# Another written-out order of the tasks between the first tiles and the first FFN

## The chip, the cores and the metric

The kernel runs on one core of a Trainium2 chip. The metric is the device time of one execution in microseconds (us). A core has five engines with a queue of instructions each: TensorE (PE: matmuls and transposes), VectorE (DVE), ScalarE (ACT), GpSimd (POOL) and SyncE (SP, which issues most transfers). An engine works through its own queue in order; between engines, semaphores say when an operand is ready or a buffer free. So the order in which a program writes its instructions is, for each engine, the order in which they run, and an instruction that waits holds up all that stand behind it.

## The reference

Two layers on 512 positions of width 1024 in float32. Each layer is a token mixer and a SwiGLU FFN; each of the four is wrapped as below, with shift, scale and gate computed from a conditioning vector c.

```
def residual_update(x, c, ada_w, ada_b, ln_g, ln_b, sublayer):
    shift, scale, gate = ada_modulation(c, ada_w, ada_b)
    out = sublayer(x * (1 + scale) + shift)
    return layer_norm(ALPHA * x + (1 + gate) * out, ln_g, ln_b)
```

The mixer of layer 0, in which the change lies, makes one input projection (q, keys and values of three branches, gates, and u and v of a gated MLP). Sparse attention with 8 query heads and 2 groups of keys takes compressed blocks of 32 positions, selected blocks of 64 (here all of them: 8 blocks, of which up to 16 may be chosen) and a window of 512, and adds the three results with a gate per head. Beside it a spatial gate computes u * (tril(W_s) norm(v) + b) in chunks of 128 positions. Both together go through one output projection:

```
    o_nsa = nsa_attention(q, *kv, gates, cmp_pos, cmp_w1, cmp_w2)
    o_gmlp = chunked_gmlp(u, v, gmlp_norm_g, gmlp_ws, gmlp_bs)
    return jnp.concatenate([o_nsa, o_gmlp], axis=-1) @ w_out
```

The mixer of layer 1 is a short gated convolution; an FFN is `(silu(gate) * up) @ w_out` with 2816 hidden columns.

## The kernel before

The 512 positions are four row tiles of 128 (t = 0 to 3). Float32 products are made of three matmuls: weights and activations are split into a high half (ScalarE, L469) and the rest (raw minus high, L473, on VectorE or GpSimd), called hi and lo, and a product is hi*hi + lo*hi + hi*lo. Such a split of half a weight unit (128x1024) is called a conversion here; for the output projections a fold (L459) multiplies the weights by a gate first.

The program has three parts: the first tiles (with an order of its own, ORDER_0), the stage between them and the first FFN, and the rest: first FFN, layer 1 and second FFN. The change is in the stage, about 60 to 304 us of the profile. What it does there: the compression of keys and values (L1054); the rest of the input projection by row tiles (L1331); the gating norm (mean L1361, centring L1366, variance L1374, an inverse square root by Newton steps over all row tiles at once, L1389 to L1397, then apply L1401 and gain L1406); the spatial-gate matmul (L1445) with its evacuation (L1449); its turn into columns (L1474) with a high half (L1482) and a low half (L1484); attention; and the output projection (L533), each piece of which is evicted into the residual by VectorE (L538).

Attention goes by units, from the last row tile to the first and through the two key groups: unit (3,0), (3,1), (2,0) down to (0,1); "V" and the numbers name a unit's value part. A unit has score heads (L1520, L1569) with a masked maximum on VectorE (L1528), exponentials on ScalarE (L1599), sums and scales by 1/sum (L1605, L1606, and L1611 on GpSimd or L1617 on ScalarE). Its compressed scores are then turned on TensorE (L1670) into a bank, split into a high half (L1673, ScalarE) and a low half (L1676, VectorE) and multiplied with the compressed values (L1680). The same is done block by block with the other scores: turn (L1693), high (L1698), low (L1702), product (L1707, L1708). Banks are scarce: two for turns, one for products of values, one for pieces of the output projection. At the end of a unit an add (L1738) and a split (L1746, L1749) give the high and low half of the mixed heads, mixh and mixl. The pieces of the output projection that read the spatial gate (gh, gl) and those that read mixh and mixl are tasks of their own and may stand anywhere behind their inputs.

Everything in the stage is a task of a planner: an object of class Plan gets, by `plan.add`, the engines on which the task could run with a cost for each, the tasks it needs, a key, and the ring buffers that it takes and gives back. A search over such orders used the costs (`run`, with a lock for pairs of VectorE and GpSimd operations). The kernel as it is built does not search; it reads a list of numbers:

```
        for z in map(int, order.split()):
            t = self.tasks[z // 4]
            fn = t.opts[z % 4][2]
            if fn:
                fn()
```

A number z stands for task z // 4 on the engine of its option z % 4. The names of buffers and the semaphores between engines follow from the order in which the tasks write their instructions. Later stages are written out by loops.

Of the kernel before, what the change touches and what calls it, by code (L numbers as in the profile page):

```python
# [2102 lines left out]
```

## Time and profile before

| | us |
|---|---|
| median of 3 runs (lowest to highest) | 1232.64 (1231.92 to 1235.42) |
| the profiled execution | 1232.91 |
| its span, first to last instruction | 1231.0 |
| mean granted clock of TensorE | 0.992 |

The profile is of one execution. The 40 slices of its page are 30.8 us each; the stage of the change is slices 2 to 9. Its engine rows, in tenths of busy time (9 is 90% or more), with the clock that TensorE was granted:

```profile
PE   7999999979999999999999999999999999999996
...
DVE  1287676887766765657656688456674353535346
...
POOL 3232021443000000000002000002010000000005
PEclk9999999989999999999999999999999999999998
```

A 9 in the row of TensorE can be 90% or 100%; the ninth slice (246 to 277 us) is the only one of the stage that shows less, in the row of TensorE and in that of the clock. In timelines, "x4" joins four neighbouring instructions of one kind, and the bracket behind a row gives how long the engine had been idle before it and what ended that.

### The profile page before, as it was taken

The page shows a single profiled execution, that of the slowest core. Times are in us where ns is not written, and L with a number is a line of the kernel's source. Part 1 is how long each engine was busy: PE and PEld are TensorE (multiplying, and loading weights), DVE is VectorE, ACT ScalarE, POOL GpSimd, SP SyncE. Part 2 cuts the span into 40 slices and gives each one's busy share as a digit, 9 for nine tenths or more (in the row PEclk, how much of TensorE's full clock was granted, in tenths as well). Part 3 has the DMA queues.
Part 4 walks back from the last instruction along what each step waited for, and adds up shares of the span by engine and source line. Part 5 has one row for each costly group of instructions (what it writes and reads, how often), then busy time and mean ns, then how long its engine had stood idle before and what let it go on. Part 6 is the DMA issues. An engine that isn't in the chain of part 4 may idle for free.

```text
span 1231.0 us, 15579 instructions
## 1 busy us (share of the span) xinstructions
PE 1199.6 (97%) x6057; PEld 980.8 (80%) x6057; DVE 764.4 (62%) x1233; ACT 437.6 (36%) x751; POOL 128.1 (10%) x230
## 2 busy tenths in 40 slices
PE   7999999979999999999999999999999999999996
PEld 5787767868988888888888988888988888888885
DVE  1287676887766765657656688456674353535346
ACT  3473276975332131313224332124433131213222
POOL 3232021443000000000002000002010000000005
PEclk9999999989999999999999999999999999999998
DMA  9785651052365554555630366330363132423301
GB/s 298 223 290 170 198 177 45 1 180 70 109 199 189 171 177 140 193 159 186 205 103 1 106 202 222 103 103 1 103 205 102 58 114 69 131 76 103 103 1 68
DMA packets 121465, 164.74 MB, mean 134 GB/s; under 512 B 5861, under 2 KB 87085, under 8 KB 121392
## 3 DMA queue, kind: packets, MB, share of 16 engines
q1 hardware_dynamic: 105552, 132.33, 34.2%
q10 hardware_dynamic: 14208, 26.75, 6.5%
q0 software_dynamic: 1632, 4.67, 1.3%
q8 instruction: 47, 0.77, 0.2%
q14 instruction: 26, 0.21, 0.1%
HBM read 161.63 MB, written 2.10 MB: 133 GB/s over the span
## 4 chain that ended last, share of the span: by engine, by line
PE 82%; DVE 2%; ACT 1%; issue 1%; POOL 0%; DVEq 0%; ACTq 0%
PE pi L521 50%; PE po L533 26%; PE ptp L1693 1%; PE ph L1520 1%; PE pt L671 1%; PE pvo L1708 1%; PE pvo L1707 1%; ACT sc L1599 1%; DVE xr L538 0%; PE aa L1155 0%; PE pa L357 0%; PE pa L361 0%; DVE bst L564 0%; DVE sc L1528 0%; PE ph L1569 0%
## 5 line engine op out<-in xcount | busy, mean ns | idle before, releaser
L521 PE MATMUL pi<-h,hi 128*128 128x512 f32 (+1 forms) x2016 | 575.9, 371 | 0.0
L521 PEld LDWEIGHTS pi<-h,hi 128*128 128x128 f32 x2016 | 365.4, 188 | 66.4 <-issue 1.6
L521 PE MATMUL pi<-h,lo 128*128 128x512 f32 (+1 forms) x1008 | 372.9, 370 | 0.0
L469 ACT ACTIVATE hi<-raw 128x1024 fp32r<-128x1024 f32 (+1 forms) x186 | 187.1, 1045 | 283.0 <-PE po L533 141.9
L473 DVE TENSOR_TENSOR lo<-raw,hi 128x1024 fp32r<-128x1024 f32 (+1 forms) x180 | 215.2, 1234 | 71.6 <-ACT hi L469 69.8
L521 PEld LDWEIGHTS pi<-h,lo 128*128 128x128 f32 x1008 | 189.8, 188 | 33.0
L533 PE MATMUL po<-hi,ah 128*128 128x512 f32 (+1 forms) x420 | 165.8, 395 | 0.3
L533 PE MATMUL po<-hi,al 128*128 128x512 f32 (+1 forms) x420 | 164.5, 392 | 0.0
L533 PE MATMUL po<-lo,ah 128*128 128x512 f32 (+1 forms) x420 | 164.3, 391 | 0.0
L538 DVE TENSOR_TENSOR xr<-xr,po 128x512 f32<-128x512 f32 x129 | 87.0, 680 | 120.3 <-PE po L533 120.2
L533 PEld LDWEIGHTS po<-hi,ah 128*128 128x128 f32 x420 | 79.0, 188 | 19.8 <-DVE xr L538 1.9
L533 PEld LDWEIGHTS po<-lo,ah 128*128 128x128 f32 x420 | 79.1, 188 | 17.8 <-issue 0.2
L533 PEld LDWEIGHTS po<-hi,al 128*128 128x128 f32 x420 | 78.9, 188 | 17.8
L1954 ACT ACTIVATE ah<-sg 128x512 fp32r<-128x512 f32 x44 | 27.8, 632 | 174.8 <-DVE sg L1999 174.8
L1999 DVE TENSOR_TENSOR sg<-sg,pi 128x512 f32<-128x512 f32 x44 | 30.2, 687 | 92.6 <-PE pi L521 92.6
L329 DVE SCALAR_TENSOR_TENSOR acc<-ar,cs,acc 128x512 f32<-128x512 f32 x98 | 73.4, 749 | 4.2 <-DMA ar<-in_ada_w_dram 2.1
L459 DVE TENSOR_TENSOR raw<-raw,gateb 128x1024 f32<-128x1024 f32 x59 | 69.5, 1218 | 1.3 <-DMA raw<-in_even_w_out_dram 1.2
L1995 ACT ACTIVATE sg<-pi 128x512 f32<-128x512 f32 x44 | 26.3, 597 | 118.2 <-PE pi L521 118.2
L1331 PE MATMUL pi<-hi,h 128*128 128x512 f32 (+1 forms) x192 | 59.7, 378 | 0.0
L1955 DVE TENSOR_TENSOR al<-sg,ah 128x512 fp32r<-128x512 f32 x44 | 30.5, 693 | 30.8 <-ACT ah L1954 30.8
L681 ACT ACTIVATE v<-pt,b,g 128x128 f32<-128x128 f32 x84 | 31.5, 455 | 43.8 <-PE pt L671 36.7
L653 POOL TENSOR_SCALAR v<-mv 128x1 f32<-128x1 f32 x9 | 2.3, 258 | 395.3 <-DVE mv L569 395.2
(264 smaller groups left out, 1206.9 us busy)
## 6 DMA issues: line engine op xcount, KB each, us to landing
raw<-in_ffn_w_in_dram SPq DMA_DIRECT2D x88, 512.0 KB, 4.6
ar<-in_ada_w_dram ACTq DMA_DIRECT2D x48, 512.0 KB, 4.5
raw<-in_ffn_w_out_dram SPq DMA_DIRECT2D x44, 512.0 KB, 4.2
ar<-in_ada_w_dram SPq DMA_DIRECT2D x24, 512.0 KB, 4.4
raw<-in_odd_w_in_dram SPq DMA_DIRECT2D x24, 512.0 KB, 4.7
raw<-in_even_w_in_dram SPq DMA_DIRECT2D x10, 512.0 KB, 5.3
aw<-in_ada_w_dram SPq DMA_DIRECT2D x8, 512.0 KB, 6.0
aw<-in_ada_w_dram SPq DMA_DIRECT2D x4, 1024.0 KB, 9.6
```

The lines of the kernel that those rows point to most:

```text
L329: dve.scalar_tensor_tensor(acc, r, cs[:, k:k + 1], acc, op0=ALU.mult, op1=ALU.add)
L459: e.tensor_tensor(z[:, k, :], z[:, k, :], gateb[fold == 2], op=ALU.mult)
L469: act(hl[0][:, i * n0:i * n0 + n0], raw(i), AF.Copy)
L473: e.tensor_tensor(hl[1][:, sl], self.raw.pop(2 * u + i), hl[0][:, sl], op=ALU.subtract)
L521: mm(p[:, sl], w, h[z][k // 4][:, k % 4, sl], start=k == 0 and i == 0, stop=k == KT - 1 and i == 2)
L533: mm(p[:, c], s_, w[:, k % 2, c0], start=first and i == 0, stop=last and i == n - 1)
L538: dve.tensor_tensor(z, z, p[:, c], op=ALU.add)
L681: act(v[:, q, :], p[:, q, :], AF.Identity, scale=g1[s][:, k:k + 1], bias=b1[s][:, k:k + 1])
L1331: mm(tiles[t], s_, w[:, q, :], start=k == 0 and z == 0, stop=k == 7 and z == 2)
L1954: act(a[0][:, k, :], f, AF.Copy)
L1955: dve.tensor_tensor(a[1][:, k, :], f, a[0][:, k, :], op=ALU.subtract)
L1999: dve.tensor_tensor(f, f, p, op=ALU.mult)
```

## The change

The text ORDER_1 is another order of the same tasks, and for some tasks another option of engine. Beside it, some 30 costs that `plan.add` is given are other numbers (durations of each task taken from a trace); `follow` does not read them. Nothing else is changed. The diff, cut:

```diff
 ORDER_1 = """
-292 64 304 392 624 288 736 864 976 281 1660 1716 1184 4180 4236 4292 4904 56 60 296 300 4 0 285
+292 64 4 1184 56 60 284 289 304 392 624 736 864 976 1660 1716 4180 296 300 4236 4292 4904 0 277
...
-        comp_in[cc] = plan.add([("act", 2.1, lambda cc=cc: compress_in(cc, None)),
-                                ("dve", 2.6, lambda cc=cc: compress_in(cc, dve))],
+        comp_in[cc] = plan.add([("act", 2.6, lambda cc=cc: compress_in(cc, None)),
+                                ("dve", 3.04, lambda cc=cc: compress_in(cc, dve))],
                                [f0_], -150, rel=[(held, MM + cc)])
...
-    nw = plan.add([("pool", 5.5, lambda: norm_newton(pool)), ("dve", 4.2, lambda: norm_newton(dve))],
+    nw = plan.add([("pool", 8.5, lambda: norm_newton(pool)), ("dve", 4.2, lambda: norm_newton(dve))],
                   var_t, -99)
...
-        a = plan.add(("pe", .87, lambda g=g: mix_pe(g)), vn_t + wsT_t[g // 4:g // 4 + 1], -103 + g,
+        a = plan.add(("pe", .4, lambda g=g: mix_pe(g)), vn_t + wsT_t[g // 4:g // 4 + 1], -103 + g,
...
-        lc = plan.add(("dve", .62, low_c), [hc], key, rel=[(tc_, "tr")])
+        lc = plan.add(("dve", .71, low_c), [hc], key, rel=[(tc_, "tr")])
...
```

What stands in the queues, before and now, at four places. In a row: the line of the kernel before, the operation, the buffers written and read, the shape; "x4" joins neighbours that read alike.

First, VectorE around the gating norm. nt are the norm's small tables, vv the values to be normed, ng the gain. Before:

```order
L1374 TENSOR_REDUCE nt_677<-sq 128x8 x2
L329 SCALAR_TENSOR_TENSOR acc<-ar,cs,acc 128x512 x2
L1184 SCALAR_TENSOR_TENSOR gateb<-pa,gb 128x512
L459 TENSOR_TENSOR raw<-raw,gateb 128x1024
L473 TENSOR_TENSOR lo<-raw,hi 128x608 x2
L1401 TENSOR_TENSOR vv<-vv,nt_679 128x512 x4
L1406 TENSOR_TENSOR vv<-vv,ng 128x512 x4
L459 TENSOR_TENSOR raw<-raw,gateb 128x1024 x3
```

Now, from the last variance on:

```order
L1374 TENSOR_REDUCE nt_677<-sq 128x8
L329 SCALAR_TENSOR_TENSOR acc<-ar,cs,acc 128x512 x2
L1389 TENSOR_SCALAR nt_677<-nt_677 128x32
L1390 TENSOR_SCALAR nt_678<-nt_677 128x32
L1391 TENSOR_SCALAR nt_679<-nt_677 128x32
L1394 TENSOR_TENSOR nt_680<-nt_679 128x32
L1395 TENSOR_TENSOR nt_680<-nt_680,nt_678 128x32
L1396 TENSOR_SCALAR nt_680<-nt_680 128x32
L1397 TENSOR_TENSOR nt_679<-nt_680,nt_679 128x32
```

The Newton steps (19 instructions, from L1389) stood in GpSimd's queue and stand now in VectorE's, between the variances and the applies; the weight folds stand partly ahead of the last gains.

Second, VectorE ahead of the low half of the compressed scores (L1676, ptc) of unit (1,1). lo<-raw,hi is a conversion, mixf the add of a unit's end. Before:

```order
L1528 ISA scc,nmx<-ph,cmask 128x32
L1528 ISA nmx 128x1
L473 TENSOR_TENSOR lo<-raw,hi 128x1024
L1738 TENSOR_TENSOR mixf<-pvo,tmp 64x256 x2
L1528 ISA sc_2499,nmx<-ph,mstrip 128x128
L1528 ISA nmx 128x1
L1676 TENSOR_TENSOR ptc_645<-ptc,ptc_645 32x512
L1702 TENSOR_TENSOR pr<-ptp,pr 128x512
```

Now:

```order
L1528 ISA sc_2563,nmx<-ph,mstrip 128x128
L1528 ISA nmx 128x1
L1528 ISA sc_2562,nmx<-ph,mstrip 128x128
L1528 ISA nmx 128x1
L1605 RECIPROCAL ls<-ls 128x8
L1606 TENSOR_TENSOR ls<-ls,gates 128x8
L1676 TENSOR_TENSOR ptc_645<-ptc,ptc_645 32x512
L1528 ISA scc,nmx<-ph,cmask 128x32
```

The conversion and the add no longer stand between the maxima and the low half; a reciprocal and its multiply (L1605, L1606) do.

Third, TensorE: the pieces of the output projection that read mixh and mixl of row tile 3 (L533). Before, the first of eight, four for each half of the columns, behind the score heads of row tile 0:

```order
L1569 MATMUL ph<-khi_638,qp 128x320
L1569 MATMUL ph<-klo_640,qp 128x320
L1569 MATMUL ph<-khi_638,qp 128x320
L1569 MATMUL ph<-klo_640,qp 128x320
L533 MATMUL po<-hi,mixh 128x512
L533 MATMUL po<-lo,mixh 128x512
L533 MATMUL po<-hi,mixl 128x512
L533 MATMUL po<-hi,mixh 128x512
L533 MATMUL po<-lo,mixh 128x512
L533 MATMUL po<-hi,mixl 128x512
L533 MATMUL po<-hi,mixh 128x512
L533 MATMUL po<-lo,mixh 128x512
```

Now, in the values of unit (2,1), between turns (L1693) and products (L1707, L1708):

```order
L1693 MATMUL ptp<-ident,sc 128x128 x4
L1707 MATMUL pvo<-pr,vpk 128x512
L1708 MATMUL pvo<-pr,vpk 128x512
L533 MATMUL po<-hi,mixh 128x512
L533 MATMUL po<-lo,mixh 128x512
L533 MATMUL po<-hi,mixl 128x512
L533 MATMUL po<-hi,mixh 128x512
L533 MATMUL po<-lo,mixh 128x512
L533 MATMUL po<-hi,mixl 128x512
L1693 MATMUL ptp<-ident,sc 128x128 x4
L1707 MATMUL pvo<-pr,vpk 128x512
L1708 MATMUL pvo<-pr,vpk 128x512
```

All eight pieces of row tile 3 stood in a row; now they begin a whole unit earlier and have turns, products or heads between them.

Fourth, GpSimd, around its conversions. sc are scores to be scaled, scc compressed scores. Before, among the scales of row tiles 1 and 0:

```order
L1749 TENSOR_TENSOR mixl<-mixf,mixh 128x256
L1611 TENSOR_TENSOR sc<-sc,ls 128x512
L473 TENSOR_TENSOR lo<-raw,hi 128x1024
L1611 TENSOR_TENSOR sc<-sc,ls 128x512
L1611 TENSOR_TENSOR sc_2499<-sc_2499,ls 128x256
L1588 TENSOR_TENSOR scc<-scc,nmx 128x128
L1611 TENSOR_TENSOR sc_2565<-sc_2565,ls 128x256
L1588 TENSOR_TENSOR scc<-scc,nmx 128x128
```

Now, from the last scales of row tile 2 on:

```order
L1611 TENSOR_TENSOR sc<-sc,ls 128x768 x2
L1588 TENSOR_TENSOR scc<-scc,nmx 128x128
L473 TENSOR_TENSOR lo<-raw,hi 128x1024 x2
L1749 TENSOR_TENSOR mixl<-mixf,mixh 128x256
L1611 TENSOR_TENSOR sc<-sc,ls 128x512 x2
L473 TENSOR_TENSOR lo<-raw,hi 128x1024
L1654 TENSOR_TENSOR scc<-scc,ls 128x128
L1588 TENSOR_TENSOR scc<-scc,nmx 128x128
```

Two conversions stand next to each other, ahead of the split of the mixed heads, and a third one follows two scales later.

## Rows read from the trace of the kernel before

**Rows 1.** The page, parts 1 and 5: an engine; a group of instructions.
```profile
PE 1199.6 (97%) x6057; PEld 980.8 (80%) x6057; DVE 764.4 (62%) x1233; ACT 437.6 (36%) x751; POOL 128.1 (10%) x230
...
L469 ACT ACTIVATE hi<-raw 128x1024 fp32r<-128x1024 f32 (+1 forms) x186 | 187.1, 1045 | 283.0 <-PE po L533 141.9
```

**Rows 2.** Busy time by stage: length, engines' busy us, clock, DMA share, GB/s.
```profile
60.00:304.00 244.00, 232.71 (x1388) 184.45 (x1386) 190.75 (x490) 149.62 (x343) 72.86 (x113) 0.99 0.44 140
200.00:304.00 104.00, 96.08 (x559) 78.98 (x557) 87.67 (x272) 75.53 (x200) 40.53 (x63) 0.97 0.21 66
304.00:1100.00 796.00, 794.32 (x3756) 660.17 (x3755) 498.41 (x617) 234.75 (x323) 21.96 (x69) 1.00 0.42 133
```

**Rows 3.** Waits of TensorE: total us, times, longest us.
```profile
PE ptp L1693 <- DVE ptc L1676: 5.1, 2, 4.2
PE po L533 <- DVE xr L538: 3.3, 3, 2.3
```

**Rows 4.** Timeline of TensorE, five places: start, us, instruction, idle time before it.
```profile
130.76 0.70 PE L1445 MATMUL pg<-vv,wsT 128*128 128x256 f32 x2 [1.51 <-DVE vv L1406]
...
160.00 1.25 PE L1474 MATMUL pu<-ident,u 128*128 128x128 f32 x8 [0.47 <-DVE gl L1484]
...
215.52 0.63 PE L1693 MATMUL ptp<-ident,sc 128*128 128x128 f32 x4 [0.92 <-DVE ptc L1676]
...
251.84 1.09 PE L1693 MATMUL ptp<-ident,sc 128*128 128x128 f32 x4 [4.19 <-DVE ptc L1676]
...
263.06 0.50 PE L533 MATMUL po<-hi,mixh 128*128 128x512 f32 x1 [2.27 <-DVE xr L538]
```

**Rows 5.** Busy time by stage, 250 to 260 us.
```profile
250.00:260.00 10.00, 8.16 (x29) 7.13 (x30) 7.02 (x30) 5.79 (x18) 1.81 (x3) 0.66 0.48 157
```

**Rows 6.** Timeline of GpSimd, first and last of 19 Newton steps.
```profile
116.87 0.64 POOL L1389 TENSOR_SCALAR nt<-nt 128x32 f32<-128x32 f32 x1 [3.49 <-DVE nt L1374]
...
125.52 0.25 POOL L1397 TENSOR_TENSOR nt<-nt,nt 128x32 f32<-128x32 f32 x1
```

**Rows 7.** Timeline of VectorE, 112 to 126 us.
```profile
112.02 0.17 DVE L1362 TENSOR_SCALAR nm<-nm 128x8 f32<-128x8 f32 x1
...
125.80 1.29 DVE L1401 TENSOR_TENSOR vv<-vv,nt 128x512 f32<-128x512 f32 x2 [2.88 <-POOL nt L1397]
```

**Rows 8.** Timeline of all engines, 157.5 to 160.5 us.
```profile
158.13 0.38 ACT L1427 ACTIVATE vpk<-pi 128x256 fp32r<-128x256 f32 x1 [2.49 <-PE pi L1331]
...
158.63 1.09 ACT L1482 ACTIVATE gh<-pu 128x512 fp32r<-128x512 f32 x2
...
158.90 0.64 PE L1155 MATMUL po<-ar,cz 128*32 128x256 f32 x8
159.26 1.29 DVE L1484 TENSOR_TENSOR gl<-pu,gh 128x512 fp32r<-128x512 f32 x2 [0.20 <-ACT gh L1482]
```

**Rows 9.** Timeline of VectorE, 246 to 267 us.
```profile
246.57 3.33 DVE L473 TENSOR_TENSOR lo<-raw,hi 128x1024 fp32r<-128x1024 f32 x1
249.82 0.84 DVE L1738 TENSOR_TENSOR mixf<-pvo,tmp 64x256 f32<-64x256 f32 x2
...
251.01 0.68 DVE L1676 TENSOR_TENSOR ptc<-ptc,ptc 32x512 fp32r<-32x512 f32 x1
...
253.97 1.22 DVE L473 TENSOR_TENSOR lo<-raw,hi 128x1024 fp32r<-128x1024 f32 x1
...
265.82 0.76 DVE L1606 TENSOR_TENSOR ls<-ls,gates 128x8 f32<-128x8 f32 x1
```

**Rows 10.** Timeline of GpSimd, 246 to 267 us.
```profile
246.44 2.37 POOL L473 TENSOR_TENSOR lo<-raw,hi 128x1024 fp32r<-128x1024 f32 x1
...
264.04 2.52 POOL L473 TENSOR_TENSOR lo<-raw,hi 128x1024 fp32r<-128x1024 f32 x1 [0.83 <-ACT hi L469]
```

**Rows 11.** DMA issue at 72.4 us; last, us from issue to landing.
```profile
w<-in_even_cmp_w_dram SPq DMA_DIRECT2D x1, 0.5 KB, 8.7
```

**Rows 12.** Timeline of TensorE, 85 to 86 us.
```profile
85.32 1.86 PE L1054 MATMUL pc<-w,G 128*64 128x128 f32 x30
```

More of the change, by code (lines that the diff above doesn't have):

```diff
@@ L947, in trunk @@
         for k in ks_:
-            xt = plan.add(("pe", .45, lambda k=k: x_turn(k)), [tn, pt, x_in[g]], k0, acq=["tr"])
+            xt = plan.add(("pe", .38, lambda k=k: x_turn(k)), [tn, pt, x_in[g]], k0, acq=["tr"])
             av = plan.add([("act", .62, lambda k=k: x_affine(k, True)),
@@ L1204, in ada @@
         sb = last if on_dve else plan.add(("act", .3, settle), [last], key, rel=[(own, ring)])
-        t = plan.add(("pe", .95 if j >= 4 else .5 if on_dve else .3, turn), [sb], key, acq=["tr"],
+        t = plan.add(("pe", .7 if j >= 4 else .5 if on_dve else .36, turn), [sb], key, acq=["tr"],
                      rel=[(first, "acc")])
@@ L1225, in trunk @@
     for br in range(2):
-        a = plan.add(("act", 1.92, lambda br=br: evac_k(br, first[2 + br], 0)), [f1_], -147 + br)
-        k_t.append(plan.add(("dve", 2.4, lambda br=br: evac_k(br, first[2 + br], 1)), [a],
+        a = plan.add(("act", 2.36, lambda br=br: evac_k(br, first[2 + br], 0)), [f1_], -147 + br)
+        k_t.append(plan.add(("dve", 2.83, lambda br=br: evac_k(br, first[2 + br], 1)), [a],
                             -147 + br, rel=[(held, MM + 2 + br)]))
@@ L1231, in q_task @@
     def q_task(mt, own, p, key, rel):
-        a = plan.add(("act", .96, lambda: evac_q(mt, p(), 0)), [own], key)
-        q_t.append(plan.add(("dve", 1.2, lambda: evac_q(mt, p(), 1)), [a], key, rel=rel))
+        a = plan.add(("act", 1.22, lambda: evac_q(mt, p(), 0)), [own], key)
+        q_t.append(plan.add(("dve", 1.41, lambda: evac_q(mt, p(), 1)), [a], key, rel=rel))
     for q in range(2):
@@ L1266, in trunk @@
     c_a = plan.add(("act", .2, lambda: comp_out(0, 1)), [c_a], -139, rel=[(c_pe, "tr")])
-    ck = plan.add(("pe", .4, lambda: compress_k(0)), [c_a], -125, acq=["tr"])
+    ck = plan.add(("pe", .2, lambda: compress_k(0)), [c_a], -125, acq=["tr"])
     a = plan.add(("act", .2, lambda: compress_k(1)), [ck], -125)
@@ L1514, in trunk @@
     opened = [plan.add((None, 0, open_ap), closing + k_t + q_t, 0)]
-    opened.append(plan.add(("pool", 1.5, masks), opened, 0))
+    opened.append(plan.add(("pool", 1.9, masks), opened, 0))
     gates_t = plan.add(("act", 1.6, open_gates), [opened[0]] + vpk_t, 0)
@@ L1534, in scores @@
         ring = "sc0" if i == 0 else "hp"
-        t_max, t_exp = .16 + L * .00104, .29 + L * .00083
+        t_max, t_exp = .08 + L * .00104, .29 + L * .00083
         un.sc, un.bank = {}, {}
@@ L1561, in scores @@
         if i == 3:
-            cin = last = plan.add(("pe", 1.8, cmp_in), [un.alloc, last], key, acq=["mm"])
+            cin = last = plan.add(("pe", .9, cmp_in), [un.alloc, last], key, acq=["mm"])
         def head(r, b):
@@ L1680, in prod_c @@
             mm(un.o, vcp[:, g, :], ptc[g], start=True, stop=False)
-        tc_ = plan.add(("pe", .45, turn_c), [un.cmp, prev and prev.turns[-1]], key,
+        tc_ = plan.add(("pe", .36, turn_c), [un.cmp, prev and prev.turns[-1]], key,
                        acq=["tr"], rel=[(un.alloc, "small")])
         hc = plan.add(("act", .48, high_c), [tc_, same and same.prod_c], key)
-        lc = plan.add(("dve", .62, low_c), [hc], key, rel=[(tc_, "tr")])
+        lc = plan.add(("dve", .71, low_c), [hc], key, rel=[(tc_, "tr")])
         un.prod_c = last = plan.add(("pe", .22, prod_c), [lc, vcp_t, prev and prev.prods[-1]], key,
@@ L1712, in values @@
             k = key + (x + 1.0) / (n + 1) * 5.8
-            t = plan.add(("pe", .45, lambda x=x: turn(x)),
+            t = plan.add(("pe", .36, lambda x=x: turn(x)),
                          [un.turns[-1]] + [un.scaled[r, kbs[x][0] + 1] for r in (0, 2)], k,
@@ L1751, in values @@
         a = plan.add(("act", .48, lower), [last], k, acq=["v", "v"])
-        b_ = plan.add(("dve", .7, add), [a], k, rel=[(un.prod_c, "pv")])
+        b_ = plan.add(("dve", .86, add), [a], k, rel=[(un.prod_c, "pv")])
         b_.rel.append(a.handles[0][1])
@@ L1836, in finish_tile @@
             fs = {}
-            tp = plan.add(("pe", .45, lambda b=b, fs=fs: fs.update(f=to_h(norm.h, t, 1, b))),
+            tp = plan.add(("pe", .38, lambda b=b, fs=fs: fs.update(f=to_h(norm.h, t, 1, b))),
                           [nm, halloc], key, acq=["tr"])
```

10 lines of the change are left out of this document (5 added, 5 removed), and 124 rows, old and new, of the table ORDER_1.

## The prediction

> **What bounds the kernel now.** I read the engines' share of the span first. TensorE is busy for 1199.6 us of the span of 1231.0 us [rows 1], so only its idle time, and time at a low clock, can be won. The table by stage comes next [rows 2]: in the stretch that the order governs (60 to 304 us) TensorE is busy for 232.71 of 244 us, so 11.3 us are idle; after 304 us it is busy for 794.32 of 796 us until 1100, so what the stage gives up or wins is passed on to the end. Third, the waits of TensorE [rows 3] and the places in its timeline where they stand [rows 4]: 1.51 us before the first spatial-gate matmul at 130.76, 0.47 at 160.00, 0.92 at 215.52, 4.19 at 251.84 and 2.27 at 263.06. These five are 9.4 of the 11.3 us. Last, the clock: from 250 to 260 us the granted clock is 0.66 [rows 5]; between the two levels, 2.4 and 1.2 GHz, that is 10 x (1 - 0.66) / 0.5 = 6.8 us at 1.2 GHz. It fell while TensorE stood idle before 251.84. 0.8 us of it were idle anyway, the other 6.0 us did 3.0 us of work: 3.0 us lost. So the order can win at most 11.3 + 3.0 = 14.3 us, 1.2% of the time.
>
> **The change part by part.** The costs in the planner do not reach the program: the method that is called (follow) reads only the numbers of the order. The matmuls are the same ones. What changes is the place of each instruction in its engine's queue and, for some tasks, the engine. I walked the new order in my head with durations of the trace, engine by engine, from one waiting point to the next.
>
> (a) Newton steps of the gating norm, from GpSimd to VectorE (first piece of order). On GpSimd the first starts at 116.87 and the last ends at 125.77 [rows 6], 8.9 us; VectorE waits for it and applies norm and gain from 125.80 [rows 7]. A small VectorE operation of this kind costs 0.17 us; 19 of them with their starts are 3.2 us at least, I take 4.2. The new queue then holds a gate (0.69), a conversion, four applies, four gains at some 0.62 each and three weight folds of 1.2 ahead of the last gain, 15.7 us in all from the end of the last variance; that is about 131.6 us on the old time scale. TensorE comes to the first spatial-gate matmul later than before, since four more projection tasks (0.68 each) and one more modulation task (0.6) stand ahead of it: 129.25 + 3.3 = 132.5. The gap goes, with less than 1 us to spare: -1.5 us. If that cover is gone it stays: 0.
>
> (b) The gate's turns (160.00). In the new order the third turn stands one modulation task, 0.64 us, behind the last projection task, while the values' evacuation (0.38), the high half (0.55) and the low half (0.65) of the gate [rows 8] come one after the other on two engines, about 1.9 us with their hand-overs. New gap 1.3 instead of 0.47: +0.8 us.
>
> (c) The turn at 215.52 waited for the low half of the compressed scores. More TensorE work (2.35 us before, 3.3 now) lies between it and the turn that starts that chain: -0.9 us.
>
> (d) The turn at 251.84. VectorE had to give the low half of the compressed scores of the second unit of row tile 1. Ahead of it in its queue stood a weight conversion of 128x1024 that took 3.33 us instead of 1.22 [rows 9], beside a GpSimd conversion from 246.44 to 248.81 [rows 10]; then an add (0.84) and a score maximum. In the new order no conversion stands there (second piece of order), and the chain is one high half (0.6), the low half 0.68 and hand-overs against about 1.5 us of TensorE work. The gap goes except for what I count under (f): -4.2 us. With the gap goes the low clock that followed it: -3.0 us. If the clock falls for another reason, 0.
>
> (e) The output-projection piece at 263.06 waited for the eviction of the half of the columns before it. The eight tasks of row tile 3, which stood in one row, four for each half, are now spread between turns and products (third piece of order), with 3.2 us of TensorE work between the end of the first half and the beginning of the second: -2.3 us.
>
> (f) New waits in the same place. Two conversions for the output projection are pulled forward by some 12 us; their high halves on ScalarE (1.05 us each on the mean, [rows 1]) stand ahead of the high half of the compressed scores of the second unit of row tile 2. From the end of its transposes: 1.4 us until ScalarE is free, 0.5 to 0.6, 0.68 and a hand-over, 2.8 us; TensorE has four score heads (0.95), a turn (0.4) and a product (0.5) in the meantime, 1.85. That is a gap of 0.9, followed by smaller ones of 0.2, 0.3 and 0.5 while the chain catches up: +1.9 us. Further on, around the first turns of row tile 1, I find 0.35, 0.4, 0.1 and 0.35: +1.2 us. Bounds: 0 each, or 4.19 once as in the old order.
>
> (g) The beginning. Three low halves go from GpSimd to VectorE there (2.40 us on the one, 1.2 on the other), 3.6 us more in VectorE's queue ahead of the key evacuations that free TensorE's banks; its wait for modulation weights around 70 us hides one. The second key evacuation I find 0.8 us ahead of its need, which any collision uses up. The compression of values moves from 85.32 [rows 12] up to about 79.7; its weight transfer takes 8.7 us [rows 11] and can be issued at 69.5, so it lands at about 78.2, 1.5 us ahead. I take +1.2 us, between 0 and 3.6.
>
> (h) GpSimd's conversions beside VectorE. The trace shows what they do to each other: VectorE's conversion that began at 246.57 ended at 249.90, 1.09 us after GpSimd's ended, and a 128x8 multiply with both inputs in SBUF took 0.76, where operations of that size take 0.17, beside another GpSimd conversion [rows 7, 9, 10]. GpSimd does nine conversions instead of six. My walk finds none of them ahead of a VectorE operation that TensorE waits for; the smallest hit seen is 0.6 us, the largest 2.1. I take +0.6 us, between 0 and 3 x 2.1.
>
> The Trainium skill, "SBUF — State Buffer", section "Who interferes with whom", says that a VectorE instruction with two SBUF inputs and a GpSimd instruction that reads SBUF exclude each other for the whole instruction, the later one being blocked. By that rule the trace agrees: the 3.33 us are 2.24 us of blocking and 1.09 us of work. It speaks against this change, since three more conversions on GpSimd can each block VectorE for up to 2.4 us, while a port that is merely shared would cost about half; by sharing, (h) would be 0.3 and the sum 0.3 us lower.
>
> Sum: -1.5 + 0.8 - 0.9 - 4.2 - 3.0 - 2.3 + 1.9 + 1.2 + 1.2 + 0.6 = -6.2 us. The profiled execution took 1232.91 us, 0.3 over the median of 1232.64, so I forecast 1226.7 us.
>
> **The rivals.**
>
> 1. The waits only change places. VectorE is busy for 87.67 of the last 104 us of the stage [rows 2], and a walk by single durations misses small delays that add up in its queue. For it: each of the five gaps is a wait for VectorE [rows 4]. Against: the new gaps I find are about 1 us, and no queue stands still for long. If the new waits are double what I count (+5.7 more) the result is 1232.4 us: no change.
>
> 2. Slower: GpSimd's conversions hold VectorE back in the last third. Four of them (two back to back, then two more) fall on 225 to 275 us, where two did before. From the point on at which three of the four find a VectorE instruction with two SBUF inputs, each costs up to 2.1 us [rows 9] in a queue that is 84% busy, TensorE stands idle for over 4 us in one place, and the clock falls again as it did before 251.84. Price: 4 x 2.1 = 8.4 less the 0.6 counted, and the 3.0 us of the clock not won: -6.2 + 7.8 + 3.0 = +4.6, 1237.5 us. Against: in the old order only one of six hits reached TensorE.
>
> 3. Almost everything is won: (f) to (h) vanish behind each other. Then -6.2 - 1.9 - 1.2 - 1.2 - 0.6 = -11.1, 1221.8 us. For it: the order is as free as before, and 0.3 us between hand-overs may be counted twice. Against: each of these waits is a chain of two engines that I can follow.
>
> 4. The change does nothing, because the beginning of the FFN is set by its weights and not by the stage: 1232.9 us. For it nothing but the transfers; against it the DMA engines' share of 0.21 from 200 to 304 us [rows 2], which leaves them time to be ahead.
>
> **How the numbers follow.** The forecast case (1223.5 to 1230) has 0.50, rival 3 0.10, rivals 1 and 4 together 0.24 (1229.5 to 1236), rival 2 0.16 (above 1236). What a measurement of this kernel can tell from no change is 0.3%, 3.7 us: faster is below 1228.9, slower above 1236.3. Of the forecast case a fifth lies above 1228.9, so faster has 0.40 + 0.10 and a tenth of rival 1's share, 0.53 in all; slower has rival 2's 0.15 and a little of rival 1, 0.16; the same has 0.31. The range of 1221.5 to 1237 leaves out a tenth on each side at most.
>
> **What would show it right or wrong.** In the profile of the changed kernel: no wait of the first spatial-gate matmul for the gain (a); a wait of about 1.3 us at the gate's third turn (b); no stretch of low granted clock between 225 and 275 us, and no wait over 2 us for the low half of compressed scores or for an eviction (d, e); a wait of about 1 us for that low half in the second unit of row tile 2 (f); idle time of TensorE in the stage of 7 us or less, against 11.3. Wrong would be: a gap of over 3 us anywhere in the stage, a second stretch at 1.2 GHz, a wait for the compression weights at about 80 us (g), or a VectorE conversion of 3 us beside a GpSimd one that TensorE waits for (h).

## The result, and the profile after

The changed kernel takes 1222.7 us, the median of four runs (1222.11 to 1223.17); the kernel before took 1233.76 us in the four runs that now stand beside it (1231.92 to 1235.42). The ratio is 0.9914, with a 95% interval of 0.9898 to 0.993, so the change is worth 10.6 us (11.1 by the two medians). The forecast was 1226.7 us, a gain of 6.2: the sign and most of the places were right, the size a little over half. The profiled execution took 1223.17 us with a span of 1221.5 us, 9.7 and 9.5 us less than before.

The page first: TensorE's busy time, against [rows 1].

```profile
PE 1197.1 (98%) x6057; PEld 978.7 (80%) x6057; DVE 762.1 (62%) x1239; ACT 438.1 (36%) x751; POOL 133.4 (11%) x221
...
L469 ACT ACTIVATE hi<-raw 128x1024 fp32r<-128x1024 f32 (+1 forms) x186 | 187.0, 1045 | 277.3 <-PE po L533 141.9
```

The windows of [rows 2] and [rows 5], after; the columns are the same.

```profile
60.00:304.00 244.00, 238.96 (x1467) 190.80 (x1466) 194.29 (x505) 156.50 (x353) 78.28 (x104) 1.00 0.45 145
200.00:304.00 104.00, 100.94 (x632) 84.16 (x631) 86.67 (x272) 82.27 (x211) 50.62 (x71) 1.00 0.25 82
304.00:1100.00 796.00, 794.38 (x3718) 658.45 (x3717) 495.12 (x612) 228.13 (x314) 21.78 (x69) 1.00 0.41 132
250.00:260.00 10.00, 8.99 (x59) 6.91 (x59) 9.80 (x56) 9.94 (x29) 6.80 (x9) 1.00 0.04 12
```

The last 800 us are as they were, and the clock stays at 1.00 where it was 0.66. Windows of fixed times hold different work in the two kernels, though, since the new one is ahead. A cleaner measure is the stage itself, from the first compression matmul (L1054) to the first of the FFN (L521). That window, before and after:

```profile
67.56:297.00 229.44, 218.15 (x1296) 171.45 (x1296) 178.75 (x465) 139.27 (x322) 63.94 (x96) 0.99 0.43 140
```
```profile
67.46:287.98 220.52, 215.48 (x1299) 168.88 (x1299) 177.89 (x476) 141.33 (x328) 69.11 (x79) 1.00 0.45 146
```

The stage is 229.44 - 220.52 = 8.92 us shorter. TensorE's idle time in it fell from 11.29 (length less busy time) to 5.04 us, -6.25, and its busy time by 2.67. The two windows do not hold quite the same matmuls. A group of four transposes of the residual (L671) stood behind the first FFN matmul before, and stands ahead of it now. Before:

```profile
297.71 0.60 PE L671 MATMUL pt<-ident,xr 128*128 128x128 f32 x4
```

The next matmul starts at 298.06, so the group takes 0.35 us of TensorE. Without it the busy time fell by 3.02 us, which is what the low clock cost by [rows 5]. The rest of the 9.5 us of span lies outside the stage: 0.1 ahead of it and 0.5 behind it, of which 0.35 are this group.

All the waits of TensorE that are left in the stage, from its timeline; they add up to the 5.04 us.

```profile
90.48 0.43 PE L1077 MATMUL pk<-hid,w 128*128 128x64 f32 x2 [0.78 <-ACT hid L1072]
...
159.19 0.63 PE L1474 MATMUL pu<-ident,u 128*128 128x128 f32 x4 [1.21 <-DVE gl L1484]
...
229.89 0.63 PE L1693 MATMUL ptp<-ident,sc 128*128 128x128 f32 x4 [0.16 <-DVE pr L1702]
...
231.98 1.29 PE L1693 MATMUL ptp<-ident,sc 128*128 128x128 f32 x8 [1.00 <-DVE ptc L1676]
...
233.46 0.47 PE L1680 MATMUL pvo<-ptc,vcp 128*128 128x512 f32 x1 [0.19 <-ACT hi L469]
...
244.77 0.51 PE L533 MATMUL po<-hi,mixh 128*128 128x512 f32 x1 [0.69 <-DVE xr L538]
...
255.45 0.63 PE L1693 MATMUL ptp<-ident,sc 128*128 128x128 f32 x4 [0.32 <-DVE ptc L1676]
...
257.08 0.47 PE L1680 MATMUL pvo<-ptc,vcp 128*128 128x512 f32 x1 [0.44 <-ACT pr L1698]
...
257.81 0.63 PE L1693 MATMUL ptp<-ident,sc 128*128 128x128 f32 x4 [0.25 <-DVE pr L1702]
```

Of [rows 3], the list of waits now has 1.3 us where 5.1 stood; none is over 1.0:

```profile
PE ptp L1693 <- DVE ptc L1676: 1.3, 2, 1.0
```

Of the five gaps of [rows 4] the gate's is left, and larger (1.21 for 0.47). In unit (2,1) there is the new gap of 1.00, at the eviction 0.69 for 2.27.

### The profile page after: what moved, and what is told of

Its sections match the earlier page's. It is cut to its first block, busy times and chain, and to the rows that moved or that the text cites. A ratio compares the mean times of both kernels' runs of the same rounds, so it can differ in the third digit from the quotient of the medians.

```text
span 1221.5 us, 15600 instructions
## 1 busy us (share of the span) xinstructions
PE 1197.1 (98%) x6057; PEld 978.7 (80%) x6057; DVE 762.1 (62%) x1239; ACT 438.1 (36%) x751; POOL 133.4 (11%) x221
## 4 chain that ended last, share of the span: by engine, by line
PE 94%; DVE 2%; ACT 2%; issue 1%; POOL 1%; DMA 0%; DVEq 0%; ACTq 0%; POOLq 0%
PE pi L521 51%; PE po L533 26%; PE pi L1331 4%; PE pi L885 2%; PE ph L1520 1%; PE ptp L1693 1%; PE pt L671 1%; PE po L1155 1%; PE pi L888 1%; PE po L885 1%; PE pg L836 1%; PE pvo L1707 1%; PE pvo L1708 1%; DMA prow<-in_ada_b_dram 0%; ACT pr L1698 0%
## 5 line engine op out<-in xcount | busy, mean ns | idle before, releaser
L521 PE MATMUL pi<-h,hi 128*128 128x512 f32 (+1 forms) x2016 | 576.0, 371 | 0.0
L521 PEld LDWEIGHTS pi<-h,hi 128*128 128x128 f32 x2016 | 365.1, 188 | 66.3 <-issue 1.8
L521 PE MATMUL pi<-h,lo 128*128 128x512 f32 (+1 forms) x1008 | 372.8, 370 | 0.0
L473 DVE TENSOR_TENSOR lo<-raw,hi 128x1024 fp32r<-128x1024 f32 (+1 forms) x177 | 210.0, 1225 | 71.3 <-ACT hi L469 69.6
L521 PEld LDWEIGHTS pi<-h,lo 128*128 128x128 f32 x1008 | 189.7, 188 | 33.1
L533 PE MATMUL po<-hi,ah 128*128 128x512 f32 (+1 forms) x420 | 165.8, 395 | 0.3
L533 PE MATMUL po<-hi,al 128*128 128x512 f32 (+1 forms) x420 | 164.5, 392 | 0.0
L533 PE MATMUL po<-lo,ah 128*128 128x512 f32 (+1 forms) x420 | 164.3, 391 | 0.0
L533 PEld LDWEIGHTS po<-hi,ah 128*128 128x128 f32 x420 | 79.0, 188 | 19.9 <-DVE xr L538 1.9
L533 PEld LDWEIGHTS po<-hi,al 128*128 128x128 f32 x420 | 78.9, 188 | 17.9
L533 PEld LDWEIGHTS po<-lo,ah 128*128 128x128 f32 x420 | 79.1, 188 | 17.7 <-issue 0.2
```

The source lines that it names most:

```text
L473: e.tensor_tensor(hl[1][:, sl], self.raw.pop(2 * u + i), hl[0][:, sl], op=ALU.subtract)
L521: mm(p[:, sl], w, h[z][k // 4][:, k % 4, sl], start=k == 0 and i == 0, stop=k == KT - 1 and i == 2)
L533: mm(p[:, c], s_, w[:, k % 2, c0], start=first and i == 0, stop=last and i == n - 1)
```

## The experiments

The kernel before ran beside each; its median was 1233.55 us beside experiments 1, 3, 4 and 5, 1233.79 beside 6 to 9, and 1232.97 beside 2, 10 and 11. Stage lengths are from the one profiled execution of each, against 229.44 us before and 220.52 after; two executions of the changed kernel differ by 0.4. Edits of the order are shown as what moves in an engine's queue, or by the numbers.

**1. One conversion alone, in the order before.** GpSimd and the rest stay.

```diff
 (VectorE's queue, unit (1,1))
 L1528 ISA scc,nmx<-ph,cmask 128x32
-L473 TENSOR_TENSOR lo<-raw,hi 128x1024
 L1738 TENSOR_TENSOR mixf<-pvo,tmp 64x256 x2
...
 L1676 TENSOR_TENSOR ptc<-ptc,ptc 32x512
 L1702 TENSOR_TENSOR pr<-ptp,pr 128x512
+L473 TENSOR_TENSOR lo<-raw,hi 128x1024
```

> The order of before with one task moved: VectorE's weight conversion of 128x1024 that stood ahead of the low half of the compressed scores of unit (1,1) now stands two low halves later. Theory (the gain is the sum of local waits, and this wait took the clock with it): the idle 4.19 us before the turn shrink by the 3.33 us of the conversion to about 0.9, no stretch at 1.2 GHz follows, and the time falls by 3.3 + 3.0 = 6.3 us. Rival A (the clock falls there for the kind of work, not for the idle time): 3.3 us less and the granted clock from 250 to 260 us stays near 0.66. Rival B (VectorE is simply short there, the wait moves on to the next low half or eviction): 1 us less or nothing.

Measured: 1230.82 us, ratio 0.9981 (0.9964 to 0.9998); the stage 228.09, 1.35 us shorter. VectorE's timeline there, and TensorE's turn:

```profile
244.20 0.08 DVE L1528 DVE_READ_ACCUMULATOR2_ANT nmx<- 128x1 f32 x1
245.73 0.85 DVE L1738 TENSOR_TENSOR mixf<-pvo,tmp 64x256 f32<-64x256 f32 x2 [1.45 <-ACT tmp L1731]
...
246.94 0.68 DVE L1676 TENSOR_TENSOR ptc<-ptc,ptc 32x512 fp32r<-32x512 f32 x1
...
247.76 0.63 PE L1693 MATMUL ptp<-ident,sc 128*128 128x128 f32 x4 [2.48 <-DVE ptc L1676]
```

The gap shrank from 4.19 to 2.48 only. VectorE now stands idle for 1.45 us itself: the add at the end of the unit before waits for ScalarE's evacuation (L1731) of the last product, and the low half stands behind the add. So the conversion held 1.7 of the 4.19 us; for the other 2.5 the suspect is the end of one unit, which stands ahead of the next in both queues. And the clock fell all the same, to 0.50 from 249 to 252 us, and again from 259 to 262, behind a wait of 2.27 us at the eviction. The step as I had put it is refuted.

**2. The end of the unit moved too.** As 1, and the high half (L1673) and low half (L1676) of unit (1,1) stand ahead of the evacuation and the add of unit (1,0).

```diff
 (VectorE's queue)
+L1676 TENSOR_TENSOR ptc<-ptc,ptc 32x512
 L1738 TENSOR_TENSOR mixf<-pvo,tmp 64x256 x2
...
-L1676 TENSOR_TENSOR ptc<-ptc,ptc 32x512
 L1702 TENSOR_TENSOR pr<-ptp,pr 128x512
```

> The order of before, with the conversion moved as in the run with one move, and in addition the high half (ScalarE) and the low half (VectorE) of the compressed scores of unit (1,1) ahead of the evacuation and the add that end unit (1,0). In the run with one move VectorE stood idle for 1.45 us for that evacuation, and 2.48 of the 4.19 us stayed. Theory (the wait had two parts, the conversion and the end of the unit before, and the clock fell for the idle time): about 0.7 us idle before the turn and 0.4 before the next product, no stretch at 1.2 GHz before 258 us, and a stage of 229.44 - 3.1 - 3.0 = 223.3 us. Rival (the clock falls for the kind of work there): 226.3 us, with the granted clock under 0.9 from 248 to 255 us.

Measured: 1229.52 us, ratio 0.9969 (0.9957 to 0.9982); the stage 227.11. TensorE's timeline, and one window of 1 us behind the last row:

```profile
248.27 0.66 PE L1693 MATMUL ptp<-ident,sc 128*128 128x128 f32 x4 [0.68 <-DVE ptc L1676]
249.24 0.47 PE L1680 MATMUL pvo<-ptc,vcp 128*128 128x512 f32 x1 [0.31 <-ACT pr L1698]
...
251.93 0.42 PE L1569 MATMUL ph<-khi,qp 128*128 128x320 f32 x1 [0.19 <-DVE nmx L1528]
...
258.88 0.50 PE L533 MATMUL po<-hi,mixh 128*128 128x512 f32 x1 [2.50 <-DVE xr L538]
```
```profile
262.00:263.00 1.00, 1.00 (x4) 0.81 (x3) 0.56 (x2) 1.00 (x2) 0.74 (x2) 0.50 1.07 376
```

The 4.19 us became 0.68 + 0.31 + 0.19 = 1.18: that part of the cause is shown, conversion and chain together. The chain's share of it is 1.3 us (2.48 to 1.18), and 1.2 us stayed. But the eviction wait of step (e) stayed too (2.50 us), and now the clock fell behind it, from 260 to 263.5 us. Both long waits had to go before the clock held; that is why this comes nearer to the rival's 226.3 us than to the 223.3 of the theory. The rival's own sign, a low clock from 248 to 255 us, is not there.

**3. A conversion from GpSimd to VectorE, in the order before**, so that the conversion ahead of the low half has no other beside it.

```diff
 ORDER_1 = """
-4204 3800 3816 2956 3804 2936 2960 3820 2880 3828 4256 2964 3808 2821 4232 3824 2844 4296 4316
+4205 3800 3816 2956 3804 2936 2960 3820 2880 3828 4256 2964 3808 2821 4232 3824 2844 4296 4316
```

> The order of before with one task's engine changed: the GpSimd conversion that ran from 246.44 to 248.81 us is done by VectorE, at its place in the order (behind VectorE's own conversion and one add, ahead of the low half). Theory (a conversion on GpSimd and one on VectorE exclude each other): VectorE's first conversion takes 1.2 instead of 3.33 us, the second 1.2; VectorE gives the low half 0.9 us earlier, so the idle time is about 3.3 us instead of 4.19. If the clock still falls after it, the time is 0.9 us lower; if not, 3.9. Rival (the 3.33 us had another cause, such as the transfers or a cold buffer): the first conversion still takes over 2 us and the idle time grows to about 5.4.

Measured: 1232.9 us, ratio 0.9991 (0.9981 to 1.0001), no change by time; the stage 228.64, gap 3.96. GpSimd's scales and VectorE's conversion:

```profile
245.25 2.04 POOL L1611 TENSOR_TENSOR sc<-sc,ls 128x512 f32<-128x512 f32 x2 [3.54 <-DVE ls L1606]
```
```profile
246.38 1.98 DVE L473 TENSOR_TENSOR lo<-raw,hi 128x1024 fp32r<-128x1024 f32 x1
248.29 0.84 DVE L1738 TENSOR_TENSOR mixf<-pvo,tmp 64x256 f32<-64x256 f32 x2
249.14 1.23 DVE L473 TENSOR_TENSOR lo<-raw,hi 128x1024 fp32r<-128x1024 f32 x1
```

I had expected 1.2 us. The scales moved into the place of the conversion: they end at 247.29, and VectorE's conversion 1.07 us later. It was held by the next GpSimd operation, which is the same rule, but my forecast for this run missed it. The gain of the stage is mostly a shorter stretch of low clock (window 250 to 260: 0.83 instead of 0.66).

**4 and 5. Each half of the new order with the other half of the old one**, cut at the low half of the compressed scores of unit (2,0), some 215 us. The first lines of the table that differ in each:

```diff
 (experiment 4: the new order up to the cut)
-292 64 304 392 624 288 736 864 976 281 1660 1716 1184 4180 4236 4292 4904 56 60 296 300 4 0 285
+292 64 4 1184 56 60 284 289 304 392 624 736 864 976 1660 1716 4180 296 300 4236 4292 4904 0 277
...
 (experiment 5: the new order behind the cut)
-2376 3448 2380 2368 2396 3428 2384 4112 2372 2329 3432 3460 2356 2408 3464 3452 3436 2392 3468
+2380 2368 2396 2384 4112 2372 2329 2356 2392 2332 2360 2400 2440 4116 2388 2452 2444 4120 2404
...
```

> The tasks that before's order has written when it comes to the low half of the compressed scores of unit (2,0) stand in the changed kernel's order and on its engines; all later tasks as before. Theory (local waits add up): the first part's own share, -1.5 and -0.4 at the spatial gate, -0.8 of two small waits up to 180 us, +0.7 at the gate's turn and +0.8 at the compressed keys: about 1.2 us less than before, 2.1 if the wait at 215.52 goes too. Rival (the changed order pays only as a whole, its first part builds up the slack that the second spends): no gain here and, with the run of the second part alone, a sum well under 9 us.

> The tasks that the changed order has written when it comes to the same low half stand in before's order and on its engines; all later tasks as in the changed kernel. Theory: -4.2 and -3.0 at the compressed scores of unit (1,1), -1.6 at the eviction, -0.4 later, +2.4 of new waits: 6.8 us less than before, 7.7 with the wait at 215.52; no stretch at 1.2 GHz after 200 us. Rival (it pays only as a whole): under 4 us.

Measured: the first half alone 1233.98 us, ratio 0.9999 (0.9987 to 1.001), the stage 1.66 us longer; the second alone 1227.25, 0.9942 (0.9925 to 0.9959), the stage 5.54 us shorter. The windows of the two stages:

```profile
68.37:299.47 231.10, 220.00 (x1294) 171.69 (x1295) 183.62 (x478) 139.04 (x321) 62.40 (x81) 0.98 0.44 138
```
```profile
67.55:291.45 223.90, 216.29 (x1298) 169.25 (x1299) 172.71 (x461) 141.03 (x328) 68.81 (x93) 1.00 0.46 142
```

The first half misses what was expected, by its seam and by the clock; the second comes near it in time (6.3 us by the medians) and falls 1.3 us short in the stage. The halves don't fit: in experiment 4 the seam has three new waits (0.41, 1.08 and 0.22 us), in 5 two (0.34 and 0.78). Idle time against before is -0.2 and -3.7 us; less the seam -1.9 and -4.8, together -6.7 against -6.25 for the whole change. In experiment 4 the clock fell behind the gap of 4.19 us and again behind the 2.28 at the eviction, 1.85 us of busy time more than before; in 5 it held, 1.86 less. So roughly three quarters of the idle time won, and all of the clock, come from the last third of the stage. By the bare lengths the rival of experiment 4 would hold, since the first half alone wins nothing and both together win 3.9 of 8.9 us; that the seam is to blame is booked from the listed waits, not shown by a run.

**6. The Newton steps back on GpSimd, in the new order.**

```diff
 ORDER_1 = """
-908 1308 1672 1688 704 1692 708 580 1340 712 1324 1696 1344 716 720 585 724 1356 1348 1328 1360
+908 1308 1672 1688 704 1692 708 580 1340 712 1324 1696 1344 716 720 584 724 1356 1348 1328 1360
```

> The changed order with the Newton steps of the norm back on GpSimd (one number). VectorE gives the last gain at 133.91 us there, just as TensorE comes to the spatial-gate matmul. The steps take 8.9 us on GpSimd instead of 3.9 on VectorE. Theory (the wait counts only for what is not covered): VectorE does its conversion and gate in the meantime, and one of its folds waits for its weights until 131.5 us in any case, so the last gain is about 0.8 us later and TensorE waits for that: +0.8 us, no stretch at 1.2 GHz. Rival (the chain through the norm is the path): the full difference, 5.0 us of idle time, and the clock falls behind it.

Measured: 1224.27 us, ratio 0.9922 (0.9907 to 0.9936); the stage 220.81, 0.29 us more than after.

```profile
134.10 0.70 PE L1445 MATMUL pg<-vv,wsT 128*128 128x256 f32 x2 [0.54 <-DVE vv L1406]
```

The gap is 0.54 us where it was 1.51, but it can't be put down to the Newton steps. Behind them VectorE stood idle for the weights of a fold that comes ahead of the last gains:

```profile
131.61 1.23 DVE L459 TENSOR_TENSOR raw<-raw,gateb 128x1024 f32<-128x1024 f32 x1 [1.46 <-DMA raw<-in_even_w_out_dram]
```

And experiments 7 and 8, with the steps on VectorE, have the same gap in the same place. In turn:

```profile
134.43 0.70 PE L1445 MATMUL pg<-vv,wsT 128*128 128x256 f32 x2 [0.50 <-DVE vv L1406]
```
```profile
135.37 0.70 PE L1445 MATMUL pg<-vv,wsT 128*128 128x256 f32 x2 [0.51 <-DVE vv L1406]
```

So the 1.51 us of step (a) went by the rest of the new order, in which TensorE comes to the spatial gate 4.3 us later than before (133.56 here, 129.25 before). That the change of engine adds anything is not shown.

**7. GpSimd's two neighbouring conversions to VectorE, in the new order.** This is the test of the slower rival: they should cost time on GpSimd, if they hold VectorE back.

```diff
 (task 1057 and task 1065, GpSimd to VectorE)
-2608 4228 3588 2644 3576 3552 2620 3592 2632 3556 3580 4304 2648 3596 4232 4280 3604 4316 4320
+2608 4229 3588 2644 3576 3552 2620 3592 2632 3556 3580 4304 2648 3596 4232 4280 3604 4316 4320
-3560 4260 3620 3608 2668 2624 3584 3612 3600 3564 4324 2676 2612 4285 4908 2692 4912 3636 3624
+3560 4261 3620 3608 2668 2624 3584 3612 3600 3564 4324 2676 2612 4285 4908 2692 4912 3636 3624
```

> The changed order with the two neighbouring GpSimd conversions (229.56 us, 4.72 us for both) back on VectorE, each at its place in the order. Theory (VectorE is the short engine from 225 to 260 us and these conversions had to leave it): 1.2 us more ahead of the low half of the compressed scores of unit (2,1), whose wait grows from 1.00 to 2.2, and 1.2 us more ahead of the next low halves: the stage is 1.5 to 2.5 us longer, more if the clock falls. Rival 2 of the prediction (GpSimd's conversions hold VectorE back): the stage gets shorter or stays.

Measured: 1225.22 us, ratio 0.993 (0.9914 to 0.9945); the stage 222.05, 1.53 longer.

```profile
233.50 1.55 PE L1693 MATMUL ptp<-ident,sc 128*128 128x128 f32 x8 [2.14 <-DVE ptc L1676]
```
```profile
235.00:240.00 5.00, 5.00 (x24) 4.42 (x24) 4.84 (x17) 4.42 (x11) 2.01 (x3) 0.72 0.45 129
```

A conversion of 1.2 us ahead of the low half makes the gap of 1.00 us 2.14, and the clock falls behind it. TensorE's idle time in the stage is 5.22 us, hardly more than the 5.04 of the change, since the waits at the eviction and at the compressed keys are not there in this run; the 1.53 us are mainly the clock. GpSimd is the right place for them, and the rival falls.

**8. The spreading of the output projection undone, in the new order.** Later pieces of row tile 3 stand in a row behind an earlier one; in the new order scores, turns and products stand between them. The eviction between the two halves moved up with them.

```diff
 (TensorE's queue; the other three pieces likewise)
 L533 MATMUL po<-hi,mixl 128x512
+L533 MATMUL po<-hi,mixh 128x512
+L533 MATMUL po<-lo,mixh 128x512
+L533 MATMUL po<-hi,mixl 128x512
...
 L1520 MATMUL ph<-khi_638,qp 128x288
...
-L533 MATMUL po<-hi,mixh 128x512
-L533 MATMUL po<-lo,mixh 128x512
-L533 MATMUL po<-hi,mixl 128x512
```

> The changed order with the four pieces of the second half of the columns of row tile 3 directly behind the four of the first half, and the eviction between them. Theory (the wait at the eviction of before goes because other TensorE work stands between the halves): TensorE waits for the eviction, 0.7 us and what stands ahead of it on VectorE, 1 to 2.3 us, and the later turns, now with less work between them, wait about as much longer; the stage is 1 to 3 us longer. Rival (the eviction is late only because of the queue on VectorE, which the other moves have cleared): 0.7 us or less.

Measured: 1226.15 us, ratio 0.9935 (0.9916 to 0.9954); the stage 223.31, 2.79 longer. The idle time is 6.45 us, 1.4 more, with new waits of 0.56 and 0.28 at later turns and the 0.51 at the spatial gate, which this edit does not touch. The other 1.4 us are busy time at an unchanged clock, and I could not place them. At the eviction TensorE waits little longer than in the change:

```profile
242.97 0.50 PE L533 MATMUL po<-hi,mixh 128*128 128x512 f32 x1 [0.78 <-DVE xr L538]
```

VectorE had nothing ahead of the eviction here: it began at 242.23, as the pieces ended, after 0.72 us of idle time. So 0.78 is the price of the eviction alone. In the kernel before, the pieces ended at 260.80 and VectorE came to the eviction 1.5 us later, which makes up the 2.27:

```profile
262.33 0.68 DVE L538 TENSOR_TENSOR xr<-xr,po 128x512 f32<-128x512 f32 x1
```

At that wait the rival is right, though not for the stage.

**9. Three waits of the new order repaired**: a modulation task moved to lie between the gate's evacuations and its third turn, and the gate's first high and low half ahead of the last evacuation of values; the low half of unit (2,1) ahead of four maxima, and its high half ahead of a ScalarE conversion; the GpSimd conversion at 239 us behind the next small multiply.

```diff
 (VectorE's queue, unit (2,1); the same idea in the two other places)
 L1702 TENSOR_TENSOR pr<-ptp,pr 128x512
+L1676 TENSOR_TENSOR ptc<-ptc,ptc 32x512
 L1528 ISA sc,nmx<-ph,mstrip 128x256
...
-L1676 TENSOR_TENSOR ptc<-ptc,ptc 32x512
 L1702 TENSOR_TENSOR pr<-ptp,pr 128x512
```

> The changed order with three of its own new waits repaired. One: at the gate's turn, one modulation task is moved behind the last projection task, and the first high and low half of the gate stand ahead of the last evacuation of values. Two: in unit (2,1) the high and low half of the compressed scores stand ahead of a conversion (ScalarE) and of four maxima (VectorE). Three: a GpSimd conversion that began at 239.07 us stands one task later, behind the product of compressed scores and weights of unit (1,0), so that VectorE's 128x8 multiply (1.55 us in the changed kernel) meets no conversion. Theory (each wait is local, its cause the queue ahead of the operation named): the idle 1.21 us fall to 0.4, 1.00 to 0 to 0.3, 0.69 to 0, the multiply takes 0.2 us; the stage is 1.8 to 2.5 us shorter than in the changed kernel (218.0 to 218.7 us from the first compression matmul to the first FFN matmul, 220.5 there). Rival (engines are short there, a repaired wait comes back at the next instruction): under 1 us.

Measured: 1220.72 us, ratio 0.9893 (0.9878 to 0.9908); the stage 218.96, 1.56 less than after. It is the fastest kernel of the study, though its interval overlaps that of the change. The waits of 1.21 and 0.69 us are gone. The third only changed places, to the next low half behind the four maxima:

```profile
231.59 0.65 PE L1693 MATMUL ptp<-ident,sc 128*128 128x128 f32 x4 [1.40 <-DVE pr L1702]
```

**10 and 11. Two of those maxima behind that low half, and the change again.** Experiment 10 is 9 with this; 11 is the changed kernel unaltered, on the same chip as 10.

```diff
 (experiment 10, VectorE's queue)
-L1528 ISA sc,nmx<-ph,mstrip 128x256 x2
 L1702 TENSOR_TENSOR pr<-ptp,pr 128x512
 L1738 TENSOR_TENSOR mixf<-pvo,tmp 64x256 x2
+L1528 ISA sc,nmx<-ph,mstrip 128x256 x2
 L1702 TENSOR_TENSOR pr<-ptp,pr 128x512
```

> The changed order with the three repairs, and the two last of the four maxima behind the next low half and the add of unit (2,0) on VectorE, since in the run with three repairs the wait of 1.00 us had become one of 1.40 for that low half. Theory (VectorE's queue ahead of one low half after the other is the cause): the 1.40 and 0.19 us fall to 0.9 together, the stage to 218.3 us. Rival (VectorE is short, what is put behind comes back as a wait for the maxima): 218.8 us or more.

> The changed kernel itself, for its time on the same chip beside the repaired ones: 1222.7 us, a stage of 220.5 us.

Measured: 10 is 1222.88 us, ratio 0.9915 (0.99 to 0.993); 11 is 1221.94, 0.9916 (0.9901 to 0.9931), and its stage of 220.14 us repeats the change within 0.4. In 10 the 1.40 us became 0.73 + 0.28 + 0.38, which is nothing won. Its stage is 221.65 us for another reason: the wait for the compressed keys was 2.32 us in that execution (0.48 in 9, 0.38 in 11, with the same instructions in that place), and the clock fell behind it:

```profile
91.62 0.43 PE L1077 MATMUL pk<-hid,w 128*128 128x64 f32 x2 [2.32 <-ACT hid L1072]
```
```profile
90.00:95.00 5.00, 3.38 (x14) 2.75 (x15) 4.55 (x10) 0.87 (x4) 0.00 (x0) 0.84 0.25 63
```

## Why the prediction came out a little over half

The idle time of the stage can be booked by the prediction's own steps, since the waits before and after are listed. What the prediction named as signs of being right is there: no wait for the gain, 1.21 us at the gate's third turn, 1.00 us in unit (2,1), no low clock from 225 to 275 us, and 5.04 us of idle time.

**What went away.** I credited 1.5 (a) + 0.9 (c) + 4.2 (d) + 2.3 (e) = 8.9 us. In fact all but the gate's 0.47 of the 11.29 us went, 10.8 us. The largest fault is here: I had read that 11.3 us are idle and that five gaps make 9.4, and gave the other 1.9 us no term. They were small waits that the timeline shows, 0.41 at 144.54, 0.20 at 172.33, 0.64 at 180.13 and 0.43 at 288.40, and 0.25 in gaps too short to be listed. The new order has none of them; no run takes them one by one. This is the largest part of the miss, 1.9 us.

**What came.** I expected 0.8 (b) + 3.1 (f) + 1.2 (g) + 0.6 (h) = 5.7 us. Measured: (b) 1.21 - 0.47 = 0.74; (f) 0.16 + 1.00 + 0.19 in unit (2,1) and 0.32 + 0.44 + 0.25 at row tile 1, 2.36; (g) 0.78, at the compressed keys, with no wait for the compression weights; (h) 0.69. Together 4.57, another 1.1 us of the miss. (b) and (f) were found where the walk put them, each smaller than forecast. (g) came behind another task than the key evacuations that I had named: the compressed keys waited for ScalarE, and ScalarE for a small copy in VectorE's queue. (h) had been an allowance without a place, so its 0.6 was near by luck.

**The clock.** -3.0 forecast; the busy time fell by 2.67, or 3.02 without the transposes that the new window has more. Net: -10.8 + 4.6 - 2.7 = -8.9 us of the stage. Of the rest up to 9.5, 0.35 are those transposes; the other 0.2 no step foresaw. The 10.6 us of the ratio are against a median of 1233.76, over the profiled execution's 1232.91.

**(a)** The wait for the gain is gone, with the margin as thin as said. The steps took 4.0 us on VectorE where I took 4.2:

```profile
117.29 0.17 DVE L1389 TENSOR_SCALAR nt<-nt 128x32 f32<-128x32 f32 x1
...
121.15 0.19 DVE L1397 TENSOR_TENSOR nt<-nt,nt 128x32 f32<-128x32 f32 x1
...
131.48 1.23 DVE L459 TENSOR_TENSOR raw<-raw,gateb 128x1024 f32<-128x1024 f32 x1 [1.73 <-DMA raw<-in_even_w_out_dram]
132.62 1.29 DVE L1406 TENSOR_TENSOR vv<-vv,ng 128x512 f32<-128x512 f32 x2
```

The last gain ends at 133.91 instead of 131.6: a fold ahead of it waits 1.73 us for its weights, which my walk did not hold. It cost nothing, since TensorE came at about 134 and not at 132.5. The size was right, but not the reason that I put first: with the Newton steps back on GpSimd (experiment 6) the 1.51 us do not return, so the order won them and not the engine.

**(d)** The gap went and the size was right, but my reason was less than half of it. I blamed the conversion; experiments 1 and 2 show 1.7 us for it and 1.3 for the end of the unit before, with 1.2 left over. The order before had both in VectorE's queue [rows 9], and the add's wait was hidden behind the conversion: the row of a long instruction does not say what the queue would have waited for without it. That the clock goes with this gap alone is refuted by experiment 2: it fell behind the eviction's wait instead. In the change both go, so the 3.0 us came out right with some luck.

**(e)** 2.27 became 0.69 instead of 0. By experiment 8, 1.5 of the 2.27 were VectorE's queue ahead of the eviction. In the change the eviction begins later still, 3.2 us behind its pieces (240.87 to 244.04), and the 3.2 us of TensorE work that the spreading put there cover all but 0.69. Without the spreading the stage is 2.8 us longer, of which 1.4 is unexplained and 0.5 stands at the spatial gate; what it is worth by itself is not settled.

**(h)** The collision was real and stood in front of an eviction. GpSimd and VectorE at 239 us, after:

```profile
239.07 3.39 POOL L473 TENSOR_TENSOR lo<-raw,hi 128x1024 fp32r<-128x1024 f32 x1
```
```profile
238.72 1.48 DVE L473 TENSOR_TENSOR lo<-raw,hi 128x1024 fp32r<-128x1024 f32 x1
...
240.93 1.55 DVE L1606 TENSOR_TENSOR ls<-ls,gates 128x8 f32<-128x8 f32 x1
...
244.04 0.68 DVE L538 TENSOR_TENSOR xr<-xr,po 128x512 f32<-128x512 f32 x1
```

VectorE's conversion ends at 240.20, and GpSimd's 2.26 us later; the 128x8 multiply ends with it, 1.55 us for 0.17 us of work, and the eviction behind comes late. In experiment 9, with GpSimd's conversion later, the same multiply took 0.17 and the 0.69 us were gone. The Trainium skill, "SBUF — State Buffer", section "Who interferes with whom", says the later of two such instructions is fully blocked; the trace agrees, in both directions: 1.13 us for GpSimd, 1.4 for VectorE.

**The rivals.** 1, 2 and 4 are out. The measured 1222.7 us lies just below the 1223.5 to 1230 of the forecast case. The price of rival 2 counted four hits of 2.1 us where its condition asks for three; three would have made 1235.4 us, under the 1236 from which I gave it its chance. Rival 2 failed because the pair of conversions met nothing that it could block: while it ran, VectorE had work with an input in a bank, at its usual durations.

```profile
229.56 4.72 POOL L473 TENSOR_TENSOR lo<-raw,hi 128x1024 fp32r<-128x1024 f32 x2 [4.05 <-ACT hi L469]
```
```profile
231.15 0.68 DVE L1676 TENSOR_TENSOR ptc<-ptc,ptc 32x512 fp32r<-32x512 f32 x1
...
231.86 0.69 DVE L1702 TENSOR_TENSOR pr<-ptp,pr 128x512 fp32r<-128x512 f32 x1
```

The same section of that page says that a VectorE instruction with at most one SBUF input does not contend with GpSimd, outside VectorE's two-port modes; these rows agree. Rival 3 named nearly the right time (1221.8) for a wrong reason: it let (f) to (h) vanish, and 3.8 of their 4.9 us stayed.
